# Products 5 and 7 of a seven-product feed-forward step in the other order

## The chip, the cores and the metric

The kernel runs on one core of a Trainium2 chip. TensorE (PE) multiplies, ScalarE (ACT) and VectorE (DVE) do the element-wise work, GpSimd (POOL) and SyncE (SP) issue transfers. The metric is the device time of one execution in microseconds; of several runs the median is taken.

## What is computed

The reference is two transformer-like blocks over 512 tokens of width 1024, the first with 16 tokens put ahead of them (528). Each block has two gated feed-forward networks (FFN) of inner width 2816 and a mixer between them; the four FFNs are where the change acts.

```python
D_MODEL = 1024
SEQ = 512
N_META = 16
D_FF = 2816
...
def swiglu(x, w_in, w_out):
    gu = x @ w_in
    return (jax.nn.silu(gu[..., :D_FF]) * gu[..., D_FF:]) @ w_out
...
def swiglu_2(x, w_gate, w_up, w_down):
    return (jax.nn.silu(x @ w_gate) * (x @ w_up)) @ w_down
...
        h = h + 0.5 * rmsnorm(swiglu(rmsnorm(h, gn[0]), ffn_w_in[i, 0], ffn_w_out[i, 0]), gn[1])
```

All arrays are float32, and the products are to have nearly float32 accuracy.

## The kernel before

**Products.** Every float32 operand is split into a high half, which is the operand rounded to the type that TensorE takes, and a low half, the rest. A product is three matmuls per 128 rows of the inner dimension: high by high, high by low, low by high. The high half of weights is cast by ACT (line 120, `whi`), the low half is the difference, which DVE takes (line 121, `wlo`).

**Stages.** An FFN handles its 22 blocks of 128 inner features in three parts (6, 8, 8 blocks), and after each part multiplies that part's features by the down weights (`dn` in the profile). In the second and third part, `Ffn.seven` computes the gates and the ups of both halves of the tokens with seven products instead of eight, in Winograd's manner: both the weights and the tokens are added and subtracted by halves beforehand, and partial sums are shared. A part of 8 blocks is called a chunk here, a block a step; 4 FFNs with 2 such chunks of 8 make 64 steps. The tokens' halves are 264 columns wide in the first FFN, 256 in the others.

**One step** has 7 products of 12 matmuls (4 blocks of 128 rows, 3 matmuls each), all at line 696. Products 1, 6, 7 and 4 add up in this order in one PSUM bank, `sa`; product 2 has a bank `sb`; products 5 and 3 add up in a bank `sc`. Between products the running sum in `sa` is copied out by ACT, since it is a partial sum of something: the first copy (`ht`, line 732) after product 1, the second (`rp`, line 744) after product 6, the third (`sqFalse`, line 753) after product 7. A copy must be over before the next product may write into `sa`. DVE adds the third copy to product 5's sum (line 755, `sqacc`). Products 4 and 3 of a step are computed one step later, while the next step's products 1, 2 and 6 run: `up_a` and `gate_b` of the step held in `old`. What follows product 4 is lines 709, 465 and 466 (the ups' features, `gh` and `gl`), what follows product 3 is lines 717, 718 (a tanh on ACT), 719, 720, 465 and 466.

**Weights.** A step needs five units: gates for products 1 and 2 (128x1024), one of 512 columns for product 6 (line 299 adds two of the loaded pieces first), one of 1024 for products 5 and 7 (in two casts), one of 512 for product 4 (ups) and one of 512 for product 3 (line 311 adds first). Whole units go through three slots in turn, 512-wide ones through four half slots. `W.release` gives a slot back and lets `W.pump` issue the next casts; `W.hold` and `tc.issue_after(last.ins)` keep the next step's units, gates first, behind the third copy on ACT's queue. Loads are issued by SP (line 99 and 93) and by POOL (line 95, which adds to what is there), two raw buffers in turn.

**Order.** The program is written in the order of `seven`, and a scheduler of the framework then orders each engine's instructions by its own estimate of when operands are ready; after that each engine runs its list strictly in order, and waits where an operand isn't ready. So PE's list interleaves products: eight matmuls of product 4 stand ahead of the first four matmuls of the next step's products 1 and 2.

Of the kernel before, what the change touches and what calls it, by code (L numbers as in the profile page):

```python
# [219 lines left out]
def two_blocks(ctx: ExitStack, tc, d, out):  # L220
# [18 lines left out]
    def ps(name="ps"):  # L239
        return psp.tile([P, 512], F32, tag="ps", name=name)  # L240
# [384 lines left out]
    def yt(tag, n):  # L625
        return sq["pool"].tile([P, 272], F32, tag=tag, bufs=2, name=tag)[:, 0:n]

    class Ffn:
# [70 lines left out]
        def seven(self, fs, below):  # L699
# [24 lines left out]
            old = None  # L724
            for f in fs:
                o = Unit(None, None)
# [20 lines left out]
                    gate_b(old)  # L747
                (u,) = W.take(1)
                o.c = ps("sc")[:, 0:n]
                self.product(o.c, u, 0, "P5", True)  # L750
                self.product(o.a, u, 1, "P7")
                m3 = yt("sqFalse", n)
                last = act.copy(out=m3, in_=o.a)  # L753
                o.c22 = yt("sqacc", n)
                dve.tensor_tensor(out=o.c22, in0=o.c, in1=m3, op=ALU.add)
                W.hold = False
# [4 lines left out]
                old = o  # L761
# [1070 lines left out]
```

## Time and profile before

| | us |
|---|---|
| median of 3 runs | 2091.21 |
| lowest and highest | 2089.55, 2098.18 |
| the profiled execution | 2091.01 |
| its span, first to last instruction | 2089.1 |
| PE busy | 2006.3 (96%) |
| DVE busy | 1549.0 (74%) |
| ACT busy | 1027.4 (49%) |
| POOL busy | 326.9 (16%) |

PE's granted clock is 0.99 of full speed over the span. The profile's times are microseconds from the span's start. PE's matmuls overlap: each is shown with a length of about 0.28 us here, while the next one starts 0.12 us later, so a busy share says little, and the distance between starts is what counts. "Idle before" is the engine's idle time just ahead of an instruction, and what ended it.

### The profile page before, as it was taken

Reading aid. Unit: us, or ns where it says so; the run is one execution under the profiler, and the core shown is the slowest. Engines: PE = TensorE matmul, PEld = TensorE weight load, DVE = VectorE, ACT = ScalarE, POOL = GpSimd, SP = SyncE. Lnnn points to the kernel's source line nnn. Section 1 sums busy time; section 2 is a strip of 40 time slices with the busy share of each in tenths; the row PEclk is TensorE's granted clock in tenths of the full one; section 3 lists DMA queues with packets and bytes.
Section 4 is the critical chain, followed back from the end, with each engine's and each line's share of the span. In section 5 each row is a group of like instructions: output and inputs, shape, how many; then the busy total and the mean of one; then the engine's idle time right before and its main releaser. Section 6 shows DMA issues by size and latency. Waiting matters only on the chain.

```text
span 2089.1 us, 34858 instructions
## 1 busy us (share of the span) xinstructions
PE 2006.3 (96%) x13583; PEld 1840.6 (88%) x13583; DVE 1549.0 (74%) x2949; ACT 1027.4 (49%) x1973; POOL 326.9 (16%) x290
## 2 busy tenths in 40 slices
PE   8999999989999999999999999998999999999998
PEld 8999999988889989989998988987777778898998
DVE  6848477787886767758777775877888877676684
ACT  5445255445555445436443543654666643353462
POOL 0011020034430002011000201103222100010200
PEclk9999999999999999999999999999999999999999
DMA  6357565222223327567532766733112153475661
GB/s 186 96 111 152 147 140 135 72 77 81 87 81 110 79 79 156 145 137 146 162 80 77 154 152 137 148 118 104 47 47 61 41 141 100 107 158 133 147 151 55
DMA packets 387851, 237.01 MB, mean 113 GB/s; under 512 B 10427, under 2 KB 383926, under 8 KB 387686
## 3 DMA queue, kind: packets, MB, share of 16 engines
q1 hardware_dynamic: 317446, 192.94, 31.4%
q0 software_dynamic: 69680, 40.62, 14.1%
q8 instruction: 106, 1.74, 0.3%
q10 hardware_dynamic: 560, 1.24, 0.2%
q14 instruction: 59, 0.48, 0.1%
HBM read 230.53 MB, written 4.23 MB: 112 GB/s over the span
## 4 chain that ended last, share of the span: by engine, by line
PE 77%; DVE 12%; ACT 5%; issue 3%; POOL 1%; DMA 1%; ACTq 0%; POOLq 0%; DVEq 0%
PE dn L484 23%; PE sa L696 17%; PE acc L484 11%; PE sc L696 8%; PE sb L696 4%; PE accB L484 3%; PE accA L484 3%; PE wo L484 2%; DVE wlo L121 1%; DVE accF L1206 1%; ACT sqFalse L753 1%; PE p L419 1%; PE ro L1604 1%; ACT whi L120 1%; DVE cv L1067 1%
## 5 line engine op out<-in xcount | busy, mean ns | idle before, releaser
L120 ACT CAST whi<-raw 128x1024 fp32r<-128x1024 f32 (+3 forms) x500 | 392.8, 801 | 360.0 <-PE dn L484 163.2
L121 DVE TENSOR_TENSOR wlo<-raw,whi 128x512 fp32r<-128x512 f32 (+2 forms) x456 | 402.3, 905 | 112.9 <-ACT whi L120 110.4
L484 PE MATMUL dn<-gh,whi 128*128 128x256 f32 (+2 forms) x908 | 277.6, 326 | 0.5 <-ACT gh L465 0.5
L484 PE MATMUL dn<-gl,whi 128*128 128x256 f32 (+2 forms) x908 | 277.7, 326 | 0.0
L484 PE MATMUL dn<-gh,wlo 128*128 128x256 f32 (+2 forms) x908 | 276.9, 325 | 0.0
L484 PE MATMUL acc<-nh,whi 128*128 128x512 f32 (+2 forms) x600 | 196.4, 361 | 8.9 <-DVE y L1212 3.9
L484 PE MATMUL acc<-nl,whi 128*128 128x512 f32 (+2 forms) x600 | 192.0, 355 | 0.0
L484 PE MATMUL acc<-nh,wlo 128*128 128x512 f32 (+2 forms) x600 | 191.6, 354 | 0.0
L484 PEld LDWEIGHTS dn<-gh,whi 128*128 128x128 f32 x908 | 163.0, 188 | 16.5 <-ACT gh L465 0.7
L484 PEld LDWEIGHTS dn<-gh,wlo 128*128 128x128 f32 x908 | 163.1, 188 | 15.0
L484 PEld LDWEIGHTS dn<-gl,whi 128*128 128x128 f32 x908 | 163.0, 188 | 15.1
L696 PE MATMUL sa<-nh,whi 128*128 128x256 f32 (+1 forms) x488 | 142.5, 292 | 24.9 <-ACT sqFalse L753 24.9
L696 PE MATMUL sc<-nh,wlo 128*128 128x256 f32 (+1 forms) x488 | 137.4, 282 | 0.0
L696 PE MATMUL sa<-nh,wlo 128*128 128x256 f32 (+1 forms) x488 | 137.3, 281 | 0.0
L696 PE MATMUL sc<-nh,whi 128*128 128x256 f32 (+1 forms) x488 | 137.2, 281 | 0.0
L696 PE MATMUL sa<-nl,whi 128*128 128x256 f32 (+1 forms) x488 | 137.1, 281 | 0.0
L696 PE MATMUL sc<-nl,whi 128*128 128x256 f32 (+1 forms) x488 | 137.0, 281 | 0.0
L484 PEld LDWEIGHTS acc<-nh,whi 128*128 128x128 f32 (+1 forms) x600 | 108.1, 194 | 25.9 <-DVE z L1054 4.5
L696 PEld LDWEIGHTS sa<-nh,whi 128*128 128x128 f32 x488 | 91.8, 188 | 34.9 <-ACT sqFalse L753 34.7
L484 PEld LDWEIGHTS acc<-nh,wlo 128*128 128x128 f32 (+1 forms) x600 | 107.0, 194 | 15.5
L484 PEld LDWEIGHTS acc<-nl,whi 128*128 128x128 f32 (+1 forms) x600 | 106.8, 193 | 13.9
L95 POOL DMA_DIRECT2D raw<-in_ffn_w_up x32 | 41.1, 1285 | 455.9 <-DMA raw<-in_ffn_w_up 245.4
(492 smaller groups left out, 5569.5 us busy)
## 6 DMA issues: line engine op xcount, KB each, us to landing
raw<-in_ffn_w_in SPq DMA_DIRECT2D x56, 512.0 KB, 3.9
raw<-in_ffn_w_gate SPq DMA_DIRECT2D x44, 512.0 KB, 3.7
raw<-in_ffn_w_in SPq DMA_DIRECT2D x64, 256.0 KB, 3.2
raw<-in_ffn_w_out SPq DMA_DIRECT2D x16, 1024.0 KB, 7.7
raw<-in_ffn_w_up SPq DMA_DIRECT2D x64, 256.0 KB, 3.3
raw<-in_ffn_w_down SPq DMA_DIRECT2D x16, 1024.0 KB, 7.2
raw<-in_a_w_in SPq DMA_DIRECT2D x18, 512.0 KB, 3.6
rawx<-in_ffn_w_in SPq DMA_DIRECT2D x32, 256.0 KB
```

Source lines behind the costliest of these rows:

```text
L95: self.nc.gpsimd.dma_start(out=dst(t), in_=src, accum_op=ALU.add)
L120: nc.scalar.copy(out=ho, in_=src)
L121: self.lo_engine.tensor_tensor(out=lw, in0=src, in1=ho.bitcast(F32), op=ALU.subtract)
L419: pe.matmul(self.p1[:, self.n:self.n + 2], lhsT=src[:, o:o + P], rhs=ones[:, 0:2], start=True, stop=True)
L484: pe.matmul(p, lhsT=w[:, k], rhs=cut(x, k, sl), start=(k == 0 and j == 0), stop=(k == last and j == 2))
L696: pe.matmul(acc, lhsT=w[:, 4 * i + k], rhs=x[:, k], start=start and k == 0 and j == 0, stop=k == 3 and j == 2, skip_group_check=not start)
L753: last = act.copy(out=m3, in_=o.a)
L1067: dve.scalar_tensor_tensor(out=v, in0=z[:, t0 + j:t0 + j + n], scalar=col(V_CW + 8 * j + c), in1=v, op0=ALU.mult, op1=ALU.add)
L1206: dve.reciprocal(out=dn, in_=dn)
L1604: pe.matmul(o[i], lhsT=vt_[:, i, j], rhs=s_[i, j][b], start=(j == 0 and b == 0), stop=(j == 3 and b == 1))
```

## The change

From the second step of a chunk on (`old` is set then), product 5 is written behind product 7 and its copy, instead of ahead of product 7. In the first step of a chunk the order stays.

```diff
                 (u,) = W.take(1)
                 o.c = ps("sc")[:, 0:n]
-                self.product(o.c, u, 0, "P5", True)
+                if not old:
+                    self.product(o.c, u, 0, "P5", True)
                 self.product(o.a, u, 1, "P7")
                 m3 = yt("sqFalse", n)
                 last = act.copy(out=m3, in_=o.a)
+                if old:
+                    self.product(o.c, u, 0, "P5", True)
                 o.c22 = yt("sqacc", n)
```

Lines behind it move down by up to three: the third copy is line 754, the sum with it line 758. What the scheduler makes of it is shown for one step in the first chunk of the third FFN.

PE, from the end of product 3 (`sc_12605`, the step before) on. Here `sc_12736` is product 5; `sa_12649` is product 7 with weights `whi2_110` and product 4 with `whi1_116`; `sa_12780` and `sb_12781` are products 1 and 2 of the next step. Before:

```order
L696 MATMUL sc_12605<-nh_81,wlo0_115 128x256
L696 MATMUL sc_12736<-nh_81,whi2_110 128x256
...
L696 MATMUL sc_12736<-nh_81,wlo2_111 128x256
L696 MATMUL sa_12649<-nh_81,whi2_110 128x256
...
L696 MATMUL sa_12649<-nh_81,wlo2_111 128x256
L696 MATMUL sa_12649<-nh_81,whi1_116 128x256
...
L696 MATMUL sa_12649<-nl_82,whi1_116 128x256
L696 MATMUL sa_12780<-xh0_11964,whi0_106 128x256
L696 MATMUL sa_12780<-xl0_11965,whi0_106 128x256
```

After:

```order
L696 MATMUL sc_12605<-nh_81,wlo0_115 128x256
L696 MATMUL sa_12649<-nh_81,whi2_110 128x256
...
L696 MATMUL sa_12649<-nh_81,wlo2_111 128x256
L696 MATMUL sc_12736<-nh_81,whi2_110 128x256
...
L696 MATMUL sc_12736<-nh_81,wlo2_111 128x256
L696 MATMUL sa_12780<-xh0_11964,whi0_106 128x256
L696 MATMUL sa_12780<-xl0_11965,whi0_106 128x256
L696 MATMUL sb_12781<-xh1_11966,whi0_106 128x256
L696 MATMUL sb_12781<-xl1_11967,whi0_106 128x256
L696 MATMUL sa_12649<-nh_81,whi1_116 128x256
```

Product 7 now stands ahead of product 5, and products 1 and 2 of the next step follow product 5 directly, where eight matmuls of product 4 stood between them and the last of these products.

ACT in the same step, from the second copy (`rp_12714`) on; `whi0_106` from 128x1024 is the next step's gates, `whi1_108` its weights for products 5 and 7. Before:

```order
L744 COPY rp_12714<-sa_12649 128x256
L718 ACTIVATE b_12729<-sqFalse_12728 128x256
L465 CAST gh_11443<-sqFalse_12728 128x256
L753 COPY sqFalse_12761<-sa_12649 128x256
L120 CAST whi0_106<-raw1_86 128x1024
L120 CAST whi1_108<-raw1_86 128x512
L120 CAST whi1_108<-rawx1_11963 128x512
L120 CAST whi0_114<-raw1_86 128x512
```

After:

```order
L744 COPY rp_12714<-sa_12649 128x256
L120 CAST whi0_114<-raw0_85 128x512
L718 ACTIVATE b_12729<-sqFalse_12728 128x256
L754 COPY sqFalse_12749<-sa_12649 128x256
L120 CAST whi0_106<-raw1_86 128x1024
L465 CAST gh_11443<-sqFalse_12728 128x256
L120 CAST whi1_108<-raw1_86 128x512
L120 CAST whi1_108<-rawx1_11963 128x512
```

The third copy and the cast of the next gates moved ahead of the cast of product 3's result (`gh_11443`), and the 512-wide cast behind the second copy.

DVE there, from line 720 on; `wlo0_107` is the low half of the next gates, `wlo1_117` in this step that of product 6's weights, `sc_12736` product 5's sum. Before:

```order
L720 SCALAR_TENSOR_TENSOR sqFalse_12728<-sqacc_12632,sqFalse_12728 128x256
L466 TENSOR_TENSOR gl_11444<-sqFalse_12728,gh_11443 128x256
L755 TENSOR_TENSOR sqacc_12763<-sc_12736,sqFalse_12761 128x256
L121 TENSOR_TENSOR wlo0_107<-raw1_86,whi0_106 128x1024
L121 TENSOR_TENSOR wlo1_109<-raw1_86,whi1_108 128x512
L299 TENSOR_TENSOR raw1_86<-raw1_86 128x512
L121 TENSOR_TENSOR wlo1_109<-rawx1_11963,whi1_108 128x512
L121 TENSOR_TENSOR wlo0_115<-raw1_86,whi0_114 128x512
L121 TENSOR_TENSOR wlo1_117<-raw1_86,whi1_116 128x512
L735 TENSOR_TENSOR a_12808<-sb_12781,ht_12794 128x256
```

After:

```order
L720 SCALAR_TENSOR_TENSOR sqFalse_12728<-sqacc_12632,sqFalse_12728 128x256
L121 TENSOR_TENSOR wlo0_107<-raw1_86,whi0_106 128x1024
L466 TENSOR_TENSOR gl_11444<-sqFalse_12728,gh_11443 128x256
L758 TENSOR_TENSOR sqacc_12763<-sc_12736,sqFalse_12749 128x256
L299 TENSOR_TENSOR raw1_86<-raw1_86 128x512
L121 TENSOR_TENSOR wlo1_109<-raw1_86,whi1_108 128x512
L121 TENSOR_TENSOR wlo1_109<-rawx1_11963,whi1_108 128x512
L121 TENSOR_TENSOR wlo1_117<-raw1_86,whi1_116 128x512
L121 TENSOR_TENSOR wlo0_115<-raw1_86,whi0_114 128x512
L735 TENSOR_TENSOR a_12808<-sb_12781,ht_12794 128x256
```

The low half of the gates moved ahead of line 466 and of the sum with the third copy; line 299 and the low half of product 6's weights moved up by one place each.

## Rows read from the trace of the kernel before

**Rows 1.** The page's first part (busy us) and the chain that ended last.

```profile
PE 2006.3 (96%) x13583; PEld 1840.6 (88%) x13583; DVE 1549.0 (74%) x2949; ACT 1027.4 (49%) x1973; POOL 326.9 (16%) x290
...
PE 77%; DVE 12%; ACT 5%; issue 3%; POOL 1%; DMA 1%; ACTq 0%; POOLq 0%; DVEq 0%
```

**Rows 2.** Waits of PE, whole span, then 100 to 400 us (us, times, longest).

```profile
PE sa L696 <- ACT sqFalse L753: 24.9, 48, 0.5
...
PE sa L696 <- ACT sqFalse L753: 6.3, 12, 0.5
```

**Rows 3.** Timeline of ACT around a chunk's second step (start, length, instruction, idle before).

```profile
1159.28 0.37 ACT L753 COPY sqFalse<-sa 128x256 f32<-128x256 f32 x1 [1.98 <-PE sa L696]
...
1169.25 0.37 ACT L753 COPY sqFalse<-sa 128x256 f32<-128x256 f32 x1 [0.59 <-PE sa L696]
1169.52 1.05 ACT L120 CAST whi<-raw 128x1024 fp32r<-128x1024 f32 x1
```

**Rows 4.** Timeline of ACT, two steps on.

```profile
1179.98 0.37 ACT L753 COPY sqFalse<-sa 128x256 f32<-128x256 f32 x1 [0.30 <-PE sa L696]
...
1188.64 0.42 ACT L718 ACTIVATE b<-sqFalse 128x256 f32<-128x256 f32 x1 [0.88 <-DVE sqFalse L717]
...
1190.72 0.37 ACT L753 COPY sqFalse<-sa 128x256 f32<-128x256 f32 x1 [0.30 <-PE sa L696]
1190.99 1.57 ACT L120 CAST whi<-raw 128x1024 fp32r<-128x1024 f32 x2
```

**Rows 5.** Timeline of PE at the end of that step.

```profile
1190.35 0.28 PE L696 MATMUL sa<-nh,wlo 128*128 128x256 f32 x1
1191.14 0.39 PE L696 MATMUL sa<-nh,whi 128*128 128x256 f32 x1 [0.52 <-ACT sqFalse L753]
1191.37 0.27 PE L696 MATMUL sa<-nl,whi 128*128 128x256 f32 x1
...
1192.17 0.31 PE L696 MATMUL sa<-xh,whi 128*128 128x256 f32 x1
```

**Rows 6.** Timeline of PE, then of ACT, at the end of a chunk.

```profile
1233.27 0.28 PE L696 MATMUL sa<-nh,wlo 128*128 128x256 f32 x1
...
1233.58 0.37 ACT L753 COPY sqFalse<-sa 128x256 f32<-128x256 f32 x1 [2.92 <-PE sa L696]
```

**Rows 7.** Timeline of ACT in the first FFN, third copies alone.

```profile
134.34 0.38 ACT L753 COPY sqFalse<-sa 128x264 f32<-128x264 f32 x1 [2.10 <-PE sa L696]
...
144.62 0.38 ACT L753 COPY sqFalse<-sa 128x264 f32<-128x264 f32 x1 [0.63 <-PE sa L696]
...
155.66 0.38 ACT L753 COPY sqFalse<-sa 128x264 f32<-128x264 f32 x1 [0.54 <-PE sa L696]
```

**Rows 8.** Timeline of DVE in the step of rows 4.

```profile
1181.34 1.82 DVE L121 TENSOR_TENSOR wlo<-raw,whi 128x1024 fp32r<-128x1024 f32 x2 [0.52 <-ACT whi L120]
...
1184.29 1.29 DVE L121 TENSOR_TENSOR wlo<-raw,whi 128x512 fp32r<-128x512 f32 x2
1185.49 0.41 DVE L735 TENSOR_TENSOR a<-sb,ht 128x256 f32<-128x256 f32 x1
...
1186.16 0.68 DVE L311 TENSOR_TENSOR raw<-raw 128x512 f32<-128x512 f32 x1
...
1187.52 0.69 DVE L121 TENSOR_TENSOR wlo<-raw,whi 128x512 fp32r<-128x512 f32 x1
1188.13 0.42 DVE L717 TENSOR_TENSOR sqFalse<-sc,rp 128x256 f32<-128x256 f32 x1
1189.09 0.42 DVE L719 SCALAR_TENSOR_TENSOR sqFalse<-b,sqFalse 128x256 f32<-128x256 f32 x1 [0.54 <-ACT b L718]
1189.55 0.43 DVE L720 SCALAR_TENSOR_TENSOR sqFalse<-sqacc,sqFalse 128x256 f32<-128x256 f32 x1
```

**Rows 9.** Timeline of POOL in that step.

```profile
1188.44 1.85 POOL L95 DMA_DIRECT2D rawx<-in_ffn_w_gate  x1
```

**Rows 10.** That step's window: us, busy us of each engine, granted clock, DMA share, GB/s.

```profile
1179.73:1190.46 10.73, 10.21 (x86) 10.01 (x84) 8.90 (x18) 6.22 (x13) 2.60 (x2) 1.00 0.81 174
```

## The prediction, made before the changed kernel ran

> **What bounds the kernel now.** I read the engine shares first, then PE's waits, then the timelines of one step. The page gives PE 96% busy and 77% of the chain that ended last [rows 1], so a change has to take time out of PE's own stream, or it moves nothing. The list of PE's waits begins with the one that this change aims at: 48 times a matmul into `sa` waits for ACT's copy of line 753, the third copy of a step; 12 of the 48 lie between 100 and 400 us, in the first FFN, whose products are 264 columns wide [rows 2]. There are 64 steps (8 chunks of 8), so 6 steps of each chunk have it: all but the first and the last.
>
> What the wait costs is best read from whole steps. ACT's third copies start at 1159.28 and 1169.25 around a step without the wait: 9.97 us. The following ones, with the wait, come 10.73 us apart (1179.98, 1190.72) [rows 3, 4]. The copy itself starts later behind the last matmul of product 7 when PE then stands still (1190.35 to 1190.72, 0.37 us) [rows 4, 5] than when PE runs on (1233.27 to 1233.58, 0.31 us) [rows 6]. So an unhindered step of 84 matmuls takes 9.97 - 0.06 = 9.91 us, 0.118 us per matmul, and the wait costs 10.73 - 9.91 = 0.82 us. In the first FFN: 10.28 - 0.06 = 10.22 us without it (0.122 us per matmul), 11.04 with it [rows 7], again 0.82. All of it: 48 x 0.82 = **39.4 us**.
>
> **The change part by part.** *Product 7 ahead of product 5.* The copy now has 12 matmuls of product 5 behind product 7 that touch neither its bank nor its result; 12 x 0.118 = 1.42 us, while the copy is over 0.31 + 0.37 = 0.68 us after product 7's last matmul started. The wait of 0.82 us goes entirely. No instruction is added or removed on any engine; SP and POOL issue the same transfers in the same order; each goes out when a cast or a DVE pass frees its buffer, so they move with those.
>
> *What is late next.* In the new order PE goes from product 5 straight to two matmuls each of the next step's products 1 and 2, and to product 4 only after those; before, eight matmuls of product 4 came in between. Products 1 and 2 need the next gates, whose cast (line 120, 128x1024) ACT still does right behind the third copy, into a slot that nobody reads any more. Count from the start of product 7's last matmul: copy at 0.31; the cast starts 0.27 later (1190.72 to 1190.99 [rows 4]), at 0.58, and takes 1.05 [rows 3], so ends at 1.63. PE resumes 0.05 us behind what it waited for (copy over at 1191.09, matmul at 1191.14) and starts the second matmul 0.23 us later, not 0.118 [rows 5]: the second matmul of product 1 starts at 1.63 + 0.05 + 0.23 = 1.91. Unhindered it would start 14 matmuls after the last of product 7, at 14 x 0.118 = 1.65. So **0.26 us of a new wait** remains in each of 36 steps; in the 12 wide ones 1.91 - 14 x 0.122 = 0.20.
>
> *The low half of the gates.* DVE starts it 0.04 us behind the cast's end, at 1.67 (with the copy at 1179.98 the cast is over at 1179.98 + 0.27 + 1.05 = 1181.30, and DVE starts at 1181.34 [rows 3, 4, 8]). It is 1.22 us long: with a 512-wide pass behind it 1.82, of which that one's own 0.69 go off, and passes overlap by 0.69 - 0.60 = 0.09, since two 512-wide ones take 1.29 [rows 8]. Over at 2.89. Its first reader is the 12th matmul behind product 5 (2+2 of products 1 and 2, 7 of product 4); it starts at 1.91 + 10 x 0.118 = 3.09 and its weights go in one matmul earlier, at 2.97. With 0.05 us to wake, 2.94 is just in time. In the wide steps only 6 matmuls of product 4 lie in between: weights wanted at 1.91 + 8 x 0.122 = 2.89, there at 2.94: 0.05 us lost, 12 times.
>
> *DVE's queue, with two passes moved behind that low half* (the step's line 466 and the sum of line 755, now 758). Each 256-wide pass takes a turn of 0.33 us (from line 735 to line 311: two in 0.67), each 512-wide one 0.60 [rows 8]. The old queue had the low half of product 6's weights over at 1184.29 + 1.29 = 1185.58, 4.24 us after the gates' low half started [rows 8]; the new one puts the two passes ahead of it and one 512-wide pass behind: 4.24 + 0.67 - 0.60 = 4.31, so it is over at 5.98. Product 6 is 37th behind product 5; its third matmul, the first to read it, starts at 1.91 + 37 x 0.118 = 6.28, its weights load at 6.16: covered by 0.13 us. Behind that come one more 512-wide pass and the rest of DVE's step, which in the old order takes 4.49 us from line 735's start (1185.49) to line 720's end (1189.55 + 0.43) [rows 8]: line 735 starts at 5.98 + 0.60 - 0.09 = 6.49, line 720 ends at 10.98. A step is now 9.91 + 0.26 = 10.17 long, so that is 0.81 into the next one, where the next low half of gates starts at 1.67: DVE has 0.8 us to spare.
>
> *The second copy* (line 744) loses product 5 as cover: only product 3's 1.42 us lie between product 6 and product 7 now. It needs the same 0.31 + 0.37 = 0.68. Priced at nothing, with 0.7 us of cover left; if ACT were busy when product 6 ends, each us beyond that would be paid 48 times.
>
> *First and last steps.* A chunk's first step keeps its order. In its last step product 7 comes after one matmul of product 5 and a down product follows; there was no wait there before. Nothing counted.
>
> **Sum.** Remaining: 36 x 0.26 + 12 x (0.20 + 0.05) = 9.4 + 3.0 = 12.4 us. Gain: 39.4 - 12.4 = **27.0 us** off the profiled execution's 2091.0 us, which is 0.2 us below the median of the three runs: 2064.0. The copy's 0.31 us rests on one kind of follower, a down product; with the other reading, 0.37, everything behind it is 0.06 later, 48 x 0.06 = 2.9 us, and the result 2066.9. The ends for the new wait are nothing (2091.0 - 39.4 = 2051.6) and the whole of the old one (2091.0). I take 0.31, since PE does run on, but half a us for small losses at the tight covers: **2064.5 us**.
>
> **The rivals.** *A: the wait is gone for good (2051.6).* It needs the cast over 0.3 us sooner. Against it: the 128x1024 casts in these steps take 1.05, and the old order already shows product 1 touching this edge: its first matmul starts at 1192.17 and is 0.31 long where others are 0.28, just behind a cast that ended at 1190.99 + 1.05 = 1192.04 [rows 4, 5]. 5%.
>
> *B: the wait comes back in part elsewhere.* The covers of 0.03 and 0.13 us are thin. If the gates' low half or product 6's weights are each late by 0.2 us more than laid out, 48 x 0.2 = 10 us per cause come back: 2068 to 2085. 15%, mostly in the lower half of that.
>
> *C: no change (2091).* The change doing nothing would need the third copy to be held until product 5 is done, by ACT's queue: ahead of it stands line 718, which waits for DVE's line 717. Line 718 starts 0.51 behind 717 (1188.13, 1188.64 [rows 4, 8]), and 717 ends 1.85 - 0.42 us before line 720 does (1188.13 to 1189.98), so line 718 is over before product 7's last matmul starts. 4%.
>
> *D: DVE becomes the bound, slower than before.* Place: the gates' low half, on which product 1 now hangs with only 11 matmuls ahead of it. If line 720 ends x us later than DVE's spare 0.8 us allow, every step is x longer; at x = 0.82 - 0.26 = 0.56 the step is as long as before, and at x = 0.8 the kernel is 48 x 0.24 = 11.5 us slower than before, 2102. Something would have to hold DVE for some 1.6 us per step. The candidate in the trace is POOL, which issues a transfer from 1188.44 to 1190.29, just while DVE does lines 717 to 720 [rows 8, 9]: if DVE had to wait it out, line 720 would end up to 1.85 us later. But those passes stand inside the issue already, with 0.42 and 0.43 us each, no longer than their like, and in the new order the issues stand beside the same passes. The Trainium skill, SBUF — State Buffer, section "SBUF: two separate sides", has a rule of this kind: a DVE pass with two SBUF inputs and a GpSimd instruction that reads SBUF hold one shared pair of ports as an exclusive lock, and the later of them blocks for the whole of the other. By that rule this rival's time would come out; the rows show no such block. 4%.
>
> *E: the transfers become the bound.* The step's DMA share is 0.81 of 10.73 us [rows 10], so 8.7 us of transfer; it decides only under a step of 8.7 us, and the new one has 9.91 + 0.26 = 10.17. Each 0.1 us beyond that costs 48 x 0.1 = 4.8 us; 10.4 to 10.8 would give 2075 to 2095. 2%.
>
> **How the numbers follow.** Forecast (2061 to 2068) 70%, A 5%, B 15%, C 4%, D 4%, E 2%. Of B two thirds lie under 2076, so 2060 to 2076 holds 0.70 + 0.10 = 8 in 10. A measurement of this kernel tells 0.5%, 10.5 us, from no change: faster means under 2080.7. Faster: forecast, A, four fifths of B and half of E, 0.70 + 0.05 + 0.12 + 0.01 = 0.88. Same: the rest of B, C and half of E, 0.03 + 0.04 + 0.01 = 0.08. Slower: D, 0.04.
>
> **What would show it.** Right: no PE wait on the third copy in the 48 steps; in its place 48 waits of product 1 (PE or its weight load, into `sa`) on line 120's cast, a lost 0.2 to 0.3 us each; third copies 10.1 to 10.2 us apart in the narrow steps, 10.4 to 10.5 in the wide ones; PE never waiting for line 744. Wrong: product 1 without a wait (A); matmuls of products 1 or 6 waiting for line 121 (B, D), with third copies over 10.7 us apart in D; line 120's casts waiting for DMA (E).

## The result, and where the time shows in the new profile

The changed kernel takes **2071.07 us** (median of 4 runs, 2070.19 to 2073.23) against 2094.07 us for the kernel before in the same comparison (2089.55 to 2098.18): a ratio of 0.9892, 95% interval 0.9867 to 0.9918. It is faster, by somewhat over 1%. The time lies inside the forecast's range of 2060 to 2076, but 6.6 us above its middle. In the two profiled executions the span, first to last instruction, went from 2089.1 to 2071.3 us, a gain of 17.8 us where 27.0 had been worked out. (That profile is of the slowest of the four runs; a second one, below, has 2069.0.) So up to a third of the expected gain went somewhere, and the rest of this document is about where.

The page's first part and the chain that ended last, of the changed kernel (answer to [rows 1]):

```profile
PE 2005.4 (97%) x13583; PEld 1838.1 (89%) x13583; DVE 1539.2 (74%) x2949; ACT 1022.8 (49%) x1973; POOL 327.1 (16%) x290
...
PE 79%; DVE 12%; ACT 4%; issue 3%; DMA 1%; POOL 0%; ACTq 0%; DVEq 0%; POOLq 0%; SPq 0%
```

PE does the same 13583 matmuls in the same busy time; only its idle time shrank. From the list of its waits, and then of those of its weight loads (engine, tile, line, what ended the wait; us in all, times, longest; answer to [rows 2]):

```profile
...
PE acc L484 <- DVE y L1215: 5.6, 2, 3.6
...
PE dn L484 <- ACT gh L465: 3.1, 2, 1.9
PE sa L696 <- ACT ht L732: 2.0, 3, 0.8
```

```profile
PEld sa L696 <- ACT whi L120: 10.7, 44, 0.3
...
PEld dn L484 <- ACT gh L465: 3.8, 2, 2.1
...
PEld sa L696 <- ACT ht L732: 2.9, 4, 1.0
...
PEld sa L696 <- ACT whiwide L120: 1.0, 4, 0.3
```

The 48 waits on the third copy (24.9 us in that list) are gone. In their place stand 48 short ones of weight loads on line 120's cast (44, and 4 whose weights lie in the slot `whiwide`), as the prediction had it. New are waits that it had not: product 6 for the first copy (line 732); and the down product's wait for `gh`, 0.5 us before, is 3.1.

One step in the third FFN, first PE at its end, then ACT (start, length, instruction, idle before; answers to [rows 4, 5]; the third copy is now line 754):

```profile
1198.62 0.28 PE L696 MATMUL sa<-nh,wlo 128*128 128x256 f32 x1
...
1200.04 0.28 PE L696 MATMUL sc<-nh,wlo 128*128 128x256 f32 x1
1200.36 0.39 PE L696 MATMUL sa<-xh,whi 128*128 128x256 f32 x1
1200.59 0.28 PE L696 MATMUL sa<-xl,whi 128*128 128x256 f32 x1
```

```profile
1198.99 0.37 ACT L754 COPY sqFalse<-sa 128x256 f32<-128x256 f32 x1 [0.42 <-PE sa L696]
1199.26 1.05 ACT L120 CAST whi<-raw 128x1024 fp32r<-128x1024 f32 x1
```

Product 7's last matmul starts at 1198.62, product 5 runs beside the copy, and product 1 starts 0.05 us behind the end of the gates' cast (1199.26 + 1.05 = 1200.31, 1200.36). The window of that step, to be put beside [rows 10] (us, then busy us of PE, PEld, DVE, ACT and POOL, granted clock, DMA share, GB/s):

```profile
1189.84:1200.05 10.21, 10.17 (x87) 9.96 (x85) 8.72 (x17) 6.09 (x14) 2.59 (x2) 1.00 0.87 176
```

10.21 us where it was 10.73, at the full granted clock in both; the DMA share rose from 0.81 to 0.87.

**Where the 27.0 us went.** I read the distances between third copies in all eight chunks off ACT's timelines, and the first and last matmul of each chunk off PE's.

- The middle steps fell from 10.73 to 10.21 us (narrow) and from 11.04 to 10.52 (wide): 0.52 us each, not the 0.56 narrow and 0.57 wide of the prediction. That makes 48 x 0.52 = 25.0 us: 2.0 short. Of it 40 steps end in another full step; they gave 20.1 of 20.8 (in the last FFN some stay at 10.23 to 10.30).
- The other 8 are the last steps of the chunks. They should have given 8 x 0.52 = 4.2 us and gave 0.2: 4.0 lost. In the table, chunk by chunk, distance of the last two third copies (before and after): those of chunks 1, 3, 5 and 7, behind which a second chunk of the same FFN follows, grew or hardly fell.
- Behind the last copies, up to the chunk's last matmul, 0.9 us more were saved.
- Between the chunks 3.4 us were lost: 1.6 behind chunk 2 and 1.9 behind chunk 6, while the other stretches balance within 0.2.

25.0 - 0.7 - 4.0 + 0.9 - 3.4 = 17.8. The 0.7 is what the 40 steps fell short of 20.8.

| chunk | 1 | 2 | 3 | 4 | 5 | 6 | 7 | 8 |
|---|---|---|---|---|---|---|---|---|
| before | 10.93 | 10.93 | 10.68 | 10.68 | 10.70 | 10.68 | 10.70 | 10.70 |
| after | 11.49 | 10.48 | 10.62 | 10.26 | 11.05 | 10.26 | 11.30 | 10.35 |

The last step of chunk 5, ACT, then PE, then SP's queue (`SPq`), and then SP's queue and ACT in the same step of the kernel before:

```profile
1209.20 0.38 ACT L754 COPY sqFalse<-sa 128x256 f32<-128x256 f32 x1 [0.42 <-PE sa L696]
...
1211.76 0.62 ACT L120 CAST whi<-raw 128x512 fp32r<-128x512 f32 x1
1213.83 1.57 ACT L120 CAST whi<-raw 128x1024 fp32r<-128x1024 f32 x2 [1.45 <-DMA raw<-in_ffn_w_down]
1215.31 0.36 ACT L732 COPY ht<-sa 128x256 f32<-128x256 f32 x1
```

```profile
1214.91 0.28 PE L696 MATMUL sc<-nh,whi 128*128 128x256 f32 x1
1215.72 0.39 PE L696 MATMUL sa<-whiwide,whi 128*128 128x256 f32 x1 [0.53 <-ACT ht L732]
```

```profile
1207.96 0.37 SPq L99 DMA_DIRECT2D raw<-in_ffn_w_down  x1
```

```profile
1220.41 0.37 SPq L99 DMA_DIRECT2D raw<-in_ffn_w_down  x1
```

```profile
1222.88 0.37 ACT L753 COPY sqFalse<-sa 128x256 f32<-128x256 f32 x1 [0.29 <-PE sa L696]
...
1226.08 1.57 ACT L120 CAST whi<-raw 128x1024 fp32r<-128x1024 f32 x2 [0.32 <-DMA raw<-in_ffn_w_down]
1227.55 0.37 ACT L732 COPY ht<-sa 128x256 f32<-128x256 f32 x1
```

In a chunk's last step ACT's list has the first cast of the *down* weights in front of the first copy. The load for it was issued at 1207.96, the cast could start only at 1213.83, and the copy behind it, which needs nothing of that load, ran at 1215.31, 6.11 us after the third copy; in the step before it was 4.46 (1198.99 to 1203.45). Product 6 waited for it. Before, the same cast stood in front of the same copy, but its load was issued 2.47 us ahead of the third copy (1220.41, 1222.88), now 1.24 us (1207.96, 1209.20); ACT waited 0.32 us for it, and PE not at all. In chunk 2 the same thing meets the down product, too. ACT and PE there:

```profile
344.51 2.00 ACT L120 CAST whi<-raw 128x1024 fp32r<-128x1024 f32 x2 [3.33 <-DMA raw<-in_ffn_w_out]
347.20 0.41 ACT L465 CAST gh<-a 128x264 fp32r<-128x264 f32 x1 [0.69 <-DVE a L709]
...
349.42 0.42 ACT L718 ACTIVATE b<-sqFalse 128x264 f32<-128x264 f32 x1
351.98 0.41 ACT L465 CAST gh<-sqFalse 128x264 fp32r<-128x264 f32 x1 [2.14 <-DVE sqFalse L720]
```

```profile
350.29 0.28 PE L484 MATMUL dn<-gh,whi 128*128 128x272 f32 x1
352.44 0.64 PE L484 MATMUL dn<-gh,whi 128*128 128x272 f32 x3 [1.86 <-ACT gh L465]
```

ACT stood idle for 3.33 us in front of two casts whose load had not landed (the trace of before has 1.33 and 1.49 us in front of such casts, and PE's gap was 0.80 instead of 2.15). The `gh` that PE then waited for is the one of 351.98; it comes out of the tanh of 349.42, which stood behind those casts and two more. The Trainium skill, TensorE: Matmul & The Clock Gate, section "Architectural detail: the array is 16× 32×32, not 1× 128×128", calls ACT's queue strictly first in, first out; these rows agree.

That was the reading of two traces. What it says of causes is tried next.

### The profile page after: what moved, and what is told of

Read it like the earlier page. It is cut to its first block, busy times and chain, and to the rows that moved or that the text cites. A ratio compares the mean times of both kernels' runs of the same rounds, so it can differ in the third digit from the quotient of the medians.

```text
span 2071.3 us, 34778 instructions
## 1 busy us (share of the span) xinstructions
PE 2005.4 (97%) x13583; PEld 1838.1 (89%) x13583; DVE 1539.2 (74%) x2949; ACT 1022.8 (49%) x1973; POOL 327.1 (16%) x290
## 3 DMA queue, kind: packets, MB, share of 16 engines
q10 hardware_dynamic: 560, 1.24, 0.2%
## 4 chain that ended last, share of the span: by engine, by line
PE 79%; DVE 12%; ACT 4%; issue 3%; DMA 1%; POOL 0%; ACTq 0%; DVEq 0%; POOLq 0%; SPq 0%
PE dn L484 24%; PE sa L696 17%; PE acc L484 12%; PE sc L696 8%; PE sb L696 4%; PE accB L484 3%; PE accA L484 3%; PE wo L484 2%; DVE wlo L121 1%; ACT whi L120 1%; DVE accF L1209 1%; PE p L419 1%; PE ro L1607 1%; DMA raw<-in_ffn_w_down 1%; DVE cv L1070 1%
## 5 line engine op out<-in xcount | busy, mean ns | idle before, releaser
L696 PE MATMUL sa<-nh,whi 128*128 128x256 f32 (+1 forms) x488 | 137.1, 281 | 0.0
L121 POOL TENSOR_TENSOR wlo<-raw,whi 128x1024 fp32r<-128x1024 f32 (+3 forms) x44 | 84.3, 1923 | 173.1 <-ACT whi L120 156.1
```

The lines of the kernel that those rows point to most:

```text
L121: self.lo_engine.tensor_tensor(out=lw, in0=src, in1=ho.bitcast(F32), op=ALU.subtract)
L696: pe.matmul(acc, lhsT=w[:, 4 * i + k], rhs=x[:, k], start=start and k == 0 and j == 0, stop=k == 3 and j == 2, skip_group_check=not start)
```

## The experiments

All times are medians; the kernel before gave 2091.6 to 2092.2 us beside them. "Narrow" and "wide" are middle steps as above.

| run | time, us | ratio (95%) | narrow | wide |
|---|---|---|---|---|
| after, again | 2071.84 | 0.9904 (0.9888 to 0.9920) | 10.21 | 10.52 |
| gates' cast halved | 2071.85 | 0.9908 (0.9894 to 0.9922) | 10.17 | 10.56 |
| last step in the old order | 2069.90 | 0.9894 (0.9881 to 0.9908) | 10.21 | 10.52 |
| product 4 early | 2067.68 | 0.9887 (0.9873 to 0.9900) | 10.05 | 10.23 |
| half loads, new order | 2084.09 | 0.9971 (0.9954 to 0.9988) | 10.21 | 10.52 |
| half loads, old order | 2113.93 | 1.0110 (1.0090 to 1.0130) | 10.73 | 11.03 |
| down casts late | 2069.35 | 0.9895 (0.9881 to 0.9910) | 10.21 | 10.53 |
| down casts late, old order | 2091.20 | 0.9996 (0.9986 to 1.0006) | 10.73 | 11.02 |
| product 4 early, down casts late | **2058.87** | 0.9848 (0.9833 to 0.9864) | 10.08 | 10.23 |
| ... and one low half moved | 2061.64 | 0.9855 (0.9840 to 0.9870) | 10.05 | 10.23 |
| ... and both low halves moved | 2059.95 | 0.9840 (0.9823 to 0.9857) | 9.97 | 10.23 |

**The changed kernel once more**, unaltered, to see whether the long last steps belong to the program.

> The changed kernel once more, unaltered, as the mark for the other kernels beside it. Its first profile: steps 10.21 us apart (narrow) and 10.52 (wide), where before had 10.73 and 11.04; last steps of chunks 10.26 to 11.49. If the long last steps and the waits at the chunks' ends are part of the program, the same steps are long again, within 0.3 us, and the span is 2071 within 2; if they were chance, other chunks show them.

They do: 11.39, 10.48, 10.62, 10.40, 10.78, 10.28, 10.76, 10.35 us, long in the same chunks, though chunk 7's is 0.54 us shorter than in the first profile, not within 0.3. The span is 2069.0, a gain of 20.1 us: the 40 steps gave 20.1 again, the last steps 0.9 instead of 0.2, and between the chunks 1.8 us were lost instead of 3.4 (1.5 behind chunk 2, 0.2 behind chunk 6). The losses in the last steps repeat, 4.0 and 3.3 us; the one behind chunk 6 does not.

**The new wait taken away: product 4 early.** Product 4 of a step is written right behind its product 5, not behind the next product 2, so that 12 matmuls stand between the third copy and product 1:

```diff
-                if old:
-                    up_a(old)
...
                 o.u2, o.u4 = W.take(2)
+                if f != fs[-1]:
+                    up_a(o)
                 old = o
```

> Product 4 of a step runs right behind its product 5 instead of between the next step's products 1 and 2 (the last step of a chunk as it was). Theory: what is left of the wait is product 1 behind the gates' cast, 0.30 us in each of 48 steps; with 12 matmuls of product 4 (1.42 us) between, the cast is over in time, and product 1 waits no more: steps 9.9 to 9.95 us (narrow), 10.2 to 10.25 (wide), 48 x 0.28 = 13.4 us less than the changed kernel, of which, as with the change itself, some of it is given back at the chunks' ends: 2057 to 2063. Rival: the low half of the gates, which DVE makes, is the next to be late; then product 1's third matmul waits, steps stay at 10.15 or more, and the time at 2068 to 2072.

The wait on line 120 is gone and the wide steps came down to 10.23, as laid out. The narrow ones stopped at 10.05 to 10.07, and the time is 4 us under that of the changed kernel (the intervals just overlap), not 13. Both the expectation and its rival missed. So either 9.91 us was wrong as the length of an undisturbed step, or another wait was left. PE at product 6's start in that kernel:

```profile
1190.53 0.28 PE L696 MATMUL sa<-whiwide,whi 128*128 128x256 f32 x1
1190.65 0.28 PE L696 MATMUL sa<-wlowide,whi 128*128 128x256 f32 x1
1190.83 0.39 PE L696 MATMUL sa<-whiwide,wlo 128*128 128x256 f32 x1
1191.05 0.28 PE L696 MATMUL sa<-whiwide,whi 128*128 128x256 f32 x1
```

The third matmul follows the second after 0.18 us instead of 0.12, is 0.39 long, and the fourth follows after 0.22: together 0.17 us, in the narrow steps only, and the list of the weight loads' waits names 3 of them, with 0.5 us in all. The weights of that third matmul are a low half that VectorE makes just before it. 10.05 to 10.08 less 0.17 is 9.88 to 9.91. Whether that is the reading is settled by the last two runs below.

**The last step in the old order.** If it is the new order itself that makes the last steps long, product 5 ahead of product 7 in them undoes it:

```diff
-                if not old:
+                late = old and f != fs[-1]
+                if not late:
                     self.product(o.c, u, 0, "P5", True)
...
-                if old:
+                if late:
                     self.product(o.c, u, 0, "P5", True)
```

> The change in all steps but the last of each chunk, which keeps product 5 ahead of product 7. Theory: the long last steps (up to 11.49 us) come from ACT's queue, where casts of the first down weights, waiting for their load, stand ahead of the first copy, on which product 6 waits; the order of products 5 and 7 there has no part in it: the same steps are long, and the time is within 3 us of the changed kernel's. Rival: the new order of the last step costs the time; then the last steps fall to 10.3 us and the time by 4 us or more, to 2067 or less.

2069.9, within 2 us of the changed kernel. The third copy of such a step comes behind 12 matmuls more; with their 1.42 us (1.46 in the wide ones) taken off, the last steps are 11.91, 10.47, 10.65, 10.40, 10.59, 10.19, 10.65 and 10.23, the pattern of the unaltered kernel. The order inside the last step has no part in it. That is not the order of the steps ahead of it, which sets when the load goes out.

**The gates' cast in two halves**, so that product 1 needs to wait only for the first:

```diff
-            return cut_of(hi, lo, 2), [(hi[:, 0:1024], lo[:, 0:1024], t[0][:, 0:1024])]
+            return cut_of(hi, lo, 2), [(hi[:, i:i + 512], lo[:, i:i + 512], t[0][:, i:i + 512]) for i in (0, 512)]
```

> The changed kernel with the gates' cast in two casts of 512 columns (and their low halves in two passes), so that the half that product 1 reads is there 0.43 us sooner; nothing else is altered by hand. Theory: product 1's wait of 0.30 us on the cast goes; product 2 or the low halves may wait for up to 0.1 us: steps 9.95 to 10.05 us (narrow), 2059 to 2065 in all. Rival: the wait is not that of the cast's length but of ACT's queue as a whole, or of DVE; then steps stay at 10.2 us or get longer, by the 0.09 us that a second cast costs ACT, and the time is 2070 to 2075.

The wait did not go, it changed its name. Weight loads of that kernel:

```profile
PEld sa L696 <- DVE wlo L121: 9.6, 44, 0.3
```

44 times again (and 4 more for `wlowide`), now for the low half of the gates, which VectorE makes behind the cast; 0.04 us won in the narrow steps, 0.04 lost in the wide ones, and the time unmoved. What stands close behind a wait sets what removing it is worth. (The profiled execution of this kernel began its first chunk 7 us later than the others; the steps and the median carry the comparison.)

**Down weights with half the bytes**, in the new and in the old order. Only the first half of each load is fetched, and both casts of it take the same bytes:

```diff
-            W.add([(view, ap[f0 * P:(f0 + nf) * P, c * 256:(c + 1) * 256].rearrange("(f p) c -> p f c", p=P))],
-                  [whole(lambda t, o=o: view(t)[:, :, o:o + P]) for o in (0, P)])
+                W.add([(lambda t: grid(t[:, 0:1024], 4),
+                        ap[f0 * P:(f0 + 4) * P, c * 256:(c + 1) * 256].rearrange("(f p) c -> p f c", p=P))],
+                      [whole(lambda t: grid(t[:, 0:1024], 8)) for o in (0, P)])
```

> The changed kernel, but of each load of down weights behind a chunk of sevens only the first half is fetched (512 KB instead of 1 MB) and cast twice, so the output is wrong; ScalarE, VectorE and TensorE have the same instructions. Theory (at a chunk's end ScalarE's queue stands at the casts of the down weights, whose load has not landed, and the first copy of the last step and the gate's casts stand behind them): the waits of those casts on the loads go, the last steps fall from 10.3-11.5 to 10.2-10.5 us, the down product no longer waits for gh (1.5-2.2 us in two chunks), and the time is 2060 to 2066 us. Rival (the long last steps come from the order of the instructions alone, whatever the loads do): last steps as in the changed kernel, time 2069 to 2073.

> The kernel before with the same half loads of down weights. Theory: its steps are 0.5 us longer, so its loads are less late and it gains less from this: 2087 to 2091 us, and the change is then worth 23 to 27 us between this kernel and the other with half loads, 48 times the 0.52 us of a step. Rival: the gain between the two stays at 18 to 21 us because what is lost lies in the stages between the chunks.

Neither time came: both kernels are *slower* than with whole loads, by 12 and 22 us, and the 29.8 us between the two say nothing of the change. Two things can still be read in the new order.

In five chunks the last step did what the theory says. The eight are 10.85, 10.46, 10.15, 10.15, 11.50, 10.15, 11.71 and 10.21 us: in chunks 2, 3, 4, 6 and 8 no wait is left. In chunk 6, where SP and POOL issue nothing else while it is under way, the half load landed 3.4 us after its issue, the whole one 5.0. In chunks 1, 5 and 7 ACT still waits for it. There the edit moved more than it was meant to: in chunk 5 three loads of the next chunk's weights went out ahead of the down load or beside it (SP at 1206.88 and 1208.73, POOL at 1210.44) that the changed kernel does not issue there, presumably into the half of a raw buffer that a half load leaves free. From issue to cast it took 6.1 us in chunk 5 with half the bytes, 5.9 with all of them. The Trainium skill, DMA: Bandwidth & Descriptors, section "Issuing engines are not separate DMA queues", says that transfers of all issuing engines interleave on the same 16 engines, which fits.

And the down product now waits for `gh` (6.0 us in 3 waits and 8.7 in 5, where the changed kernel has 3.1 in 2). The scheduler gave ACT another order: in chunk 5 a `gh` cast that stood ahead of the next cast of down weights (1222.86 and 1226.91 in the changed kernel) now stands behind it, and that cast waits for its load. ACT with half loads:

```profile
1229.85 1.04 ACT L120 CAST whi<-raw 128x1024 fp32r<-128x1024 f32 x1 [3.88 <-DMA raw<-in_ffn_w_down]
1230.80 0.40 ACT L470 CAST gh<-sqFalse 128x256 fp32r<-128x256 f32 x1
```

That is the fault of the last steps in another place. The next runs move the instruction and leave the loads alone.

**The down weights' casts behind the first copy** in a chunk's last step, in the new and in the old order. Nothing else moves in the old order: PE's list is that of before, row for row.

```diff
+            with self.behind() if self.behind and len(self.raws[r][0]) == 1 else nullcontext():
                 for ho, lw, src in splits:
...
-                act.copy(out=m1, in_=o.a)
+                m1c = act.copy(out=m1, in_=o.a)
+                W.behind = f == fs[-1] and (lambda: tc.issue_after(m1c.ins))
```

> The changed kernel with the casts of the down weights put behind the first copy in the last step of each chunk. Theory (the place in ScalarE's queue is what makes a late load cost time): product 6 of the last step no longer waits for the first copy, last steps of 10.2 to 10.6 us in all eight chunks, time 2066 to 2069. Rival (the transfers bound the chunk's end whatever the order): the same microseconds come back as waits of the down product for the weights or for gh, time 2070 to 2073.

> The kernel before (product 5 ahead of product 7 in every step) with the casts of the down weights behind the first copy in the last step, as in the run of the changed kernel with that alone (2069.4 us); TensorE's order is that of before. Theory (the change made the last step meet the loads of the down weights; before, its longer steps hid them): before loses nothing at that place, last steps stay at 10.68 to 10.93 us, time 2089 to 2093 us. Rival (the place of those casts costs both kernels the same): this kernel gains 2 to 3 us as the changed one did, 2087 to 2090, with last steps under 10.6.

This one holds. ACT in the last step of chunk 5, new order:

```profile
1213.21 0.62 ACT L121 CAST whi<-raw 128x512 fp32r<-128x512 f32 x1 [0.75 <-DVE raw L300]
1213.74 0.37 ACT L733 COPY ht<-sa 128x256 f32<-128x256 f32 x1
1214.01 2.00 ACT L121 CAST whi<-raw 128x1024 fp32r<-128x1024 f32 x2
```

The first copy (line 733 here) runs 4.5 us behind the third copy, as in every other step, not 6.1, and the cast behind it finds its load landed. The last steps:

| chunk | 1 | 2 | 3 | 4 | 5 | 6 | 7 | 8 |
|---|---|---|---|---|---|---|---|---|
| new order, casts late | 10.50 | 10.47 | 10.16 | 10.16 | 10.16 | 10.16 | 10.25 | 10.18 |
| old order, casts late | 10.94 | 10.94 | 10.66 | 10.68 | 10.68 | 10.68 | 10.70 | 10.70 |

In the new order the sum falls from 85.8 to 82.0 us: of the 4.2 us due, 4.0 have now arrived. No wait of the down product for `gh` is left among the larger ones. The chunks from first to last matmul gained 2.7 us against the first profile of the changed kernel and 2.0 against the second. The median fell by 1.7 and 2.5 us, which these few runs can't tell from nothing; the steps carry the claim. In the old order the same edit changes nothing, neither a last step nor the time. So before, the load went out early enough; the change used up that lead and gave 3 to 4 us of its own gain back there.

The lead is the same in every chunk: issue to third copy 2.47 to 2.76 us before, 1.22 to 1.33 in the new order, 1.2 to 1.4 less. The shorter step explains only 0.5 of it. The rest is that the load goes out later behind the third copy ahead of it, 8.97 us instead of 8.25 in chunk 5: it follows the end of DVE's last pass on the buffer (1207.24 + 0.69 = 1207.93, load at 1207.96), and DVE's passes did not move up with the third copy, which product 5 no longer precedes.

**Both together: product 4 early, down casts late.** Since product 4's weights now come free a step earlier, the first down cast would be issued before the last step begins; it is held back until the first copy:

```diff
+            if self.no_down and len(self.raws[r][0]) == 1:
+                break
...
+                W.no_down = f in fs[-2:]
...
+                W.no_down = f == fs[-2]
+                W.behind = f == fs[-1] and (lambda: tc.issue_after(m1c.ins))
```

> Product 4 early, right behind product 5, and the casts of the down weights behind the first copy of the last step. Theory: the gains add up, last steps near 10.2 us, time 2062 to 2066, faster than either alone. Rival (the chunk's end is bound by the transfers): as with product 4 early alone, 2066 to 2069.

2058.9 us, lower than the 2062 expected and 12 us under the changed kernel; the intervals stand apart. It beats both kernels of this study, and the two runs that follow can't be told from it. Every chunk saves 3.6 to 4.5 us against before, evenly. Of the 8.1 us of span between this and product 4 early alone, 3.4 lie in the chunks and 3.6 in the stretch behind chunk 2. There the down product's wait for `gh` of 1.3 us is gone; PE's list of the mixer is the same in both, but its granted clock was 0.50 from 412.4 to 415.8 us, 477.2 to 480.6 and 518.2 to 521.6 with product 4 early alone, and 1.00 at those places here. That part is not shown to be the edit's.

**Is 9.91 us the pace when nothing waits?** Two runs on top of that kernel, both moving VectorE's low halves. The first moves one:

```diff
-                    self.lo_engine.tensor_tensor(out=lw, in0=src, in1=ho.bitcast(F32), op=ALU.subtract)
+                    with self.tc.issue_after(self.three) if make.__name__ == "twos" and i else nullcontext():
+                        low = self.lo_engine.tensor_tensor(out=lw, in0=src, in1=ho.bitcast(F32), op=ALU.subtract)
+                    if make.__name__ == "three":
+                        self.three = low.ins
```

> Product 4 early and the down weights' casts late, as in the fastest run so far (2058.9 us), and on VectorE the low half for product 6 ahead of the second low half for product 7; nothing else moves. Theory (a narrow step of 10.08 is 84 matmuls at 0.118 = 9.91 and 0.17 that product 6's third matmul stands for its weight's low half, 0.06 of waiting and 0.11 of a matmul that could not overlap its weight load): narrow steps of 9.91 to 9.95, time 2051 to 2055 us. Rival (the engine's own pace is 10.05 when nothing waits, the 0.22 us row is no consequence of the wait): steps stay at 10.03 or more, time 2056 to 2060.

The narrow steps stayed. But the edit had missed: with the second low half for product 7 moved back, the scheduler put the one for the next product 4 in its place, and product 6's was still third. VectorE and then PE in that kernel:

```profile
1187.85 1.89 DVE L125 TENSOR_TENSOR wlo<-raw,whi 128x512 fp32r<-128x512 f32 x3
```

```profile
1189.62 0.28 PE L703 MATMUL sa<-wlowide,whi 128*128 128x256 f32 x1
1189.80 0.39 PE L703 MATMUL sa<-whiwide,wlo 128*128 128x256 f32 x1
```

Its pass is the third of the three in this row; it ends at 1187.85 + 1.89 = 1189.74, and PE goes on at 1189.80. With both moved back:

```diff
-                    with self.tc.issue_after(self.three) if make.__name__ == "twos" and i else nullcontext():
+                    with self.tc.issue_after(self.three) if make.__name__ == "ups" or make.__name__ == "twos" and i else nullcontext():
```

> As the run before it (product 4 early, down weights' casts late), but VectorE now makes the low half for product 6 ahead of both the low half for the next product 4 and the second low half for product 7; in the run before the low half for the next product 4 had only taken the place of the moved one, so that product 6's was no earlier. Theory: the low half is ready some 0.2 to 0.3 us earlier, product 6's third matmul follows the second after 0.12 instead of 0.18 and the fourth the third after 0.12 instead of 0.22, narrow steps of 9.91 to 9.95 us, time 2052 to 2057. Rival (TensorE has this pause at a change of product whatever VectorE does): narrow steps stay at 10.03 or more, time 2057 to 2062.

```profile
1197.88 0.28 PE L703 MATMUL sa<-wlowide,whi 128*128 128x256 f32 x1
1198.00 0.28 PE L703 MATMUL sa<-whiwide,wlo 128*128 128x256 f32 x1
1198.12 0.28 PE L703 MATMUL sa<-whiwide,whi 128*128 128x256 f32 x1
```

```profile
1194.97 0.28 PE L703 MATMUL sa<-xl,whi 128*128 128x256 f32 x1
1195.09 0.35 PE L703 MATMUL sa<-xh,wlo 128*128 128x256 f32 x1
1195.28 0.28 PE L703 MATMUL sa<-xh,whi 128*128 128x256 f32 x1
```

Product 6's pause is gone, whole, the 0.22 with it: the rival, that PE makes this pause by itself, falls. The steps are 9.97 us; the next short stop is already there, at product 1's third matmul, the first to read the gates' low half (VectorE's pass on it ends at 1195.00): it is 0.35 long, and the next one follows after 0.18. 9.97 - 0.06 = 9.91. The steps came within 0.04 us of what was expected; the time did not, it stayed at 2060. In the profiled execution, the slowest of four, 4.4 us were saved in the chunks, and the stretches around them took 10.9 more: behind chunk 6 the down product waits 2.3 us for `gh` (0.8 in the run before), and after that stop PE's granted clock is 0.50 from 1353.1 to 1356.4 us. Why `gh` came later was not followed up.

## Why the prediction was right, and which steps of it failed

**The range, right with some luck.** The time lies in the range of 2060 to 2076, but above the 2061 to 2068 that the forecast gave to its own mechanism. The range reached further because of rival B, which came true in kind and not in place.

**The old wait, right.** 0.82 us a step rested on an undisturbed step of 9.91 us (narrow) and 10.22 (wide). The run with product 4 early has wide steps of 10.23 without any wait, the last run narrow ones of 9.97 with 0.06 us of one. Both figures stand.

**The new wait, right in place and cause, too small by 0.04 to 0.05.** Predicted were 48 waits of product 1 on the gates' cast, 0.26 us narrow and 0.25 wide with its low half; measured 10.21 - 9.91 = 0.30 and 10.52 - 10.22 = 0.30. The mis-sized term is the copy's 0.31 us behind product 7's last matmul: it was 0.37 (1198.62 to 1198.99), though PE runs on. The prediction had tied the two values to whether PE stands still. They are tied to something else, which the trace of before shows as well. Line 753 before, line 754 after (line, engine, instruction, times; length in ns: least, median, most; first and last start):

```profile
L753 ACTq EVENT_SEMAPHORE  x48: 17/17/17, 144.6 to 2016.1; - x48
```

```profile
L754 ACTq EVENT_SEMAPHORE  x48: 17/17/17, 143.3 to 1997.2; - x48
```

48 of the 64 third copies, those of a chunk's second to seventh step, have a wait instruction of their own in front of them, which starts 0.31 us behind the matmul; the copy follows 0.06 later, whether PE stands still (before) or runs on (after). The first and last copy of a chunk have none and start at 0.31 to 0.33, whether ACT was idle for 3 us ahead of them (before) or for 0.1 (some last steps with product 4 early). The change leaves these instructions where they were. The prediction had named 0.37 as the other reading, at 2066.9 us; that reading was the right one. Cost: 2.0 us.

**"First and last steps: nothing counted", wrong.** This is the step that failed: 4.0 us in the last steps (3.3 in the second profile). The prediction looked at PE's waits of before, found none there and took the place for free. It did not ask what else was due at a time of its own. The load of the first down weights takes 5.9 us from issue to cast in the new order and 5.7 in the old (1220.41 to 1226.08), but its lead over the third copy fell from 2.47 to 1.24 us, and in ACT's list a copy that PE needs stands behind the cast that waits for it. The runs with those casts moved show it from both sides. The prediction had the means: it wrote that each transfer goes out when a cast or a DVE pass frees its buffer, and it had DVE's queue laid out, but it did not carry the two to the chunk's end.

**The stretches between chunks, not looked at: 3.4 us in one profile, 1.8 in the other, and not shown to be the change's.** Two waits of the down product for `gh` grew or appeared: in chunk 6 by 1.26 and 0.94 us in the two profiles, in chunk 2 by 1.3 us in the first and not at all in the second. They went with the down casts moved, so they belong to the same cause. Much of the rest goes with PE's clock. In the first profile the stop of 2.15 us in chunk 2 is followed, 1.5 us on, by 3.4 us at a granted clock of 0.50, the lower of its two levels, 1.2 GHz (window; columns as in the window above):

```profile
353.90:357.30 3.40, 3.40 (x18) 3.40 (x17) 3.36 (x6) 2.53 (x5) 0.00 (x0) 0.50 0.02 5
```

The 272-wide matmuls start 0.23 us apart there, 0.13 right behind, which makes some 1.5 us. The second profile has 1.00 at that place and 0.50 from 412.7 to 419.5. How much such spells shift is best seen where no order changed: the old order with the down casts late has PE's list of before row for row, and its stretch behind chunk 2 is 3.2 us longer than before's, that behind chunk 6 1.4 shorter.

The list of waits misleads here. PE's wait in the mixer behind chunk 2 for VectorE's `y` is 3.6 us in the changed kernel and 2.0 before, but it is 3.6 in that old-order run, too. It is 2.0 to 2.1 in the eight profiles in which PE ran at 0.50 for 3.4 us some 20 us ahead of it (before: 565.1 to 568.5) and 3.6 in the other five: PE came later, and waited less for the same `y`. Nothing is lost by it.

**Second copy, VectorE's spare time, product 6's low half: right.** No wait on line 744, and no narrow step was longer than 10.30 us, no wide one longer than 10.52, except at a chunk's end. The covers were as thin as laid out: the low half for product 6, given 0.13 us of cover, became the next wait as soon as product 4 was moved.

**The rivals.** A (wait gone, 2051.6) did not come. Of B's range, 2068 to 2085, the time holds the lower end; B's mechanism (the gain comes back in part elsewhere) is what happened, but at the chunks' ends and not at the low halves it named. E, the transfers, was priced by a step's DMA share (0.81, now 0.87) and given 2%: right for the middle steps, wrong for a chunk's end, where one load's latency counts and not the share. C and D fell: the 48 waits are gone, and 264-wide and 256-wide passes of VectorE kept their lengths.

## What to carry to other kernels

When a loop's step gets shorter, look at what is due at the loop's end and does not get shorter with it: the first load of the next stage, and what stands behind its consumer in an engine's queue. Put a copy that the busy engine needs ahead of a cast that may wait for a transfer; that cost nothing here and returned 3.8 us in the last steps, of the 4.0 that the change had lost there. And before forecasting the gain of a removed wait, list the two or three waits next behind it: each of those removed here uncovered another of up to 0.3 us a step. And compare repeated steps rather than spans: two profiles of one kernel differed by 1.6 us between the chunks and by less than 0.1 in the 40 middle steps together.

## What the runs showed of the hardware

- **A weight load that waits costs 0.11 us beyond its wait.** A matmul whose weight load had to wait, for the weights or for the bank, is 0.39 us long instead of 0.28, and the next one follows it after 0.22 to 0.23 us, not 0.12: before, after and with product 4 early (1191.14 and 1191.37 in [rows 5], 1200.36 and 1200.59, 1190.83 and 1191.05). The Trainium skill, TensorE: Matmul & The Clock Gate, section "Step-by-step: what each phase is for", says that PE pulls weight loads ahead of running matmuls; these rows show what was lost where one had to wait. It makes 48 x 0.11 = 5.3 us of the old wait's 39.4, about what the list of the weight loads' waits (34.7 us) lacks of it; the list of PE's has 24.9.
- **Short stops don't reach the lists.** Product 6's pause of 0.17 us, with product 4 early, cost 5 to 6 us over the narrow steps; the list of waits has 3 of them, in the next kernel none. Only the distances between matmul starts show it.
- **A wait instruction in front of a copy costs 0.06 us.** ACT's third copies start 0.31 to 0.33 us behind the start of the last matmul that they need, and 0.37 to 0.38 where a semaphore instruction of their own stands in front of them and ACT is free, before, after and with product 4 early.
- **PE's granted clock is not even between the chunks.** Spells of 3.4 us and more at 0.50 lie at other places in each profile, and with them a stretch came out 1.4 us shorter or 3.2 longer with PE's list unaltered. The middle steps compared here ran at 1.00.
